# A batched matmul on one core: weights of four matrices in one load of 24 KB runs, their casts in quarter-lane pieces shared between VectorE and ScalarE

## Chip, cores, metric

One Trainium2 chip, one core, the other cores idle. The metric is the device time of one execution in microseconds (us), median of several. The kernel before takes 519.6 us, and its executions lie within 0.3 us.

## The reference

```python
b1, b2, m, k, n = 8, 16, 256, 512, 384
x:      (8, 16, 256, 512) float32
weight: (8, 16, 512, 384) float32
out = np.matmul(x, weight)            # 128 independent products, float32
```

The kernel reads 67.1 MB of x and 100.7 MB of weights and writes 50.3 MB. The products are made in bf16.

## The kernel before

Four matrices are a group, and there are 32 groups. SyncE issues all transfers, in program order: for group n + 4 the x and the two halves of the weights, then the store of group n. ScalarE casts x to bf16 and copies the products out of PSUM. TensorE transposes x and multiplies. VectorE casts the weights to bf16 and copies the transposed x.

```python
G = 4; C = P // G; R = G * M // P; T = R // 2      # P = 128, R = 8 rows a partition, T = 4
D = 2; S = 2; HP = P // D; NG = B // G             # half loads, half lanes, 32 groups
XS, WS, OS = 2, 2 * G // D, 4                      # buffers: x, half weights, out

def load(e, t, U, s):                              # SyncE
    n = t * U + s
    e.wait_ge(x_cast, n + (1 - XS))                # cut: only for n >= XS
    e.dma_start(x_sb[s % XS], ...)                 # 2 MB, 16 KB runs
    for d in range(G // D):
        e.wait_ge(w_cast, n * (G * S) + ((d + 1) * D * S - 2 * G * S))
        e.dma_start(w_sb[slot], ...)               # 1.5 MB, 12 KB runs, two matrices

def prepare(e, t, U, s):                           # VectorE
    for d in range(G // D):
        e.wait_ge(w_in[slot], ...)
        for a in range(D):
            for h in range(S):                     # 8 casts of 64 x 1536
                e.tensor_copy(out=w_bf[...][h * HP : (h + 1) * HP],
                              in_=w_sb[slot][a * HP : (a + 1) * HP, h * KO : (h + 1) * KO, :]
                              ).then_inc(w_cast, 1)
    for q in range(T):                             # 4 copies of the transposed x
        e.wait_ge(t_made, n * T + (q + 1 + BIAS))
        e.tensor_copy(out=x_t[...], in_=pt[...]).then_inc(t_copied, 1)

def step(t, U, s, more):                           # ScalarE
    for q in range(T):
        copy_out(e, t, U, s, q)                    # PSUM -> out_sb
        if q == 1 and more:
            cast_x(e, t, U, s + 1)                 # 2 casts of 128 x 2048
```

## Time and profile before

| | kernel before |
|---|---|
| time, us | 519.6 (519.5 to 519.8) |
| busy: VectorE, ScalarE, TensorE | 63%, 41%, 61% |
| packets' share of the DMA engines | 99.2% |
| issue to landing, us: x, half weights, store | 25.9, 27.6, 30.5 |

The prediction below shows the page's lines for this. Four groups of work are needed besides (columns: line, engine, operation, out<-in, shapes, count, busy us, mean ns, idle before and its releaser):

```profile
L148 DVE CAST w_bf<-w_sb 64x1536 bf16<-64x1536 f32 x256 | 244.4, 955 | 179.4 <-DMA w_sb<-in_weight_dram 172.3
...
L195 ACT COPY out_sb<-po 128x768 f32<-128x768 f32 x128 | 99.4, 803 | 291.0 <-PE po L181 291.0
...
L130 ACT CAST x_bf<-x_sb 128x2048 bf16<-128x2048 f32 x64 | 118.5, 1902 | 6.3 <-DMA x_sb<-in_x_dram 6.3
...
L154 DVE COPY x_t<-pt 128x1024 bf16<-128x1024 bf16 x128 | 79.5, 682 | 1.0
```

VectorE waits 172 us for weights and ScalarE 291 us for products: both have time to spare.

The **packet records** have size, start and duration of every DMA packet. The **landing records** have, for each transfer, one entry for each of the 16 DMA engines. From them I take when a transfer landed on the slowest engine (the last of 16, for which the program waits) and on the median engine (the eighth). The difference is called the **lag**. The records don't number the engines, so the last at one landing need not be the last at another; the table under e14 shows where that matters.

### The profile page before, as it was taken

The numbers are of one execution on the slowest core, as the hardware profiler recorded it, in microseconds if no ns is written. First come the engines' busy times: TensorE is split into PE (matmuls) and PEld (weight loads), VectorE is DVE, ScalarE is ACT, GpSimd is POOL, SyncE is SP. The second block draws the span as 40 slices with busy tenths as digits, with TensorE's granted clock in tenths as the row PEclk, the third lists the DMA queues.
The fourth block names the chain that finished last, engine by engine and source line by source line (L and its number), as shares of the span: only waits on it lengthen the run. The fifth ranks groups of instructions, "written<-read, shape, count | busy, mean of one in ns | idle before, by whom it ended". The sixth has DMA issues, their size and how long they took to land.

```text
span 518.0 us, 11228 instructions
## 1 busy us (share of the span) xinstructions
PE 315.0 (61%) x4608; PEld 198.0 (38%) x4608; DVE 323.9 (63%) x384; ACT 212.8 (41%) x193; POOL 0.7 (0%) x6
## 2 busy tenths in 40 slices
PE   0685775476655676555756557665566655675654
PEld 0453443343433443333434334343344333343432
DVE  0878867655577555775556765557755577555670
ACT  3073643455234552335542345423455234553242
POOL 0000000000000000000000000000000000000000
PEclk9798976888668776868786687768777787878687
DMA  8999999999999999999999999999999999999995
GB/s 337 430 424 428 426 429 427 430 428 427 430 429 426 431 425 430 428 430 432 426 427 429 430 433 425 427 430 428 432 429 427 427 430 430 430 429 424 432 428 229
DMA packets 18868, 218.16 MB, mean 421 GB/s; under 512 B 2096, under 2 KB 2096, under 8 KB 2608
## 3 DMA queue, kind: packets, MB, share of 16 engines
q1 hardware_dynamic: 18864, 218.11, 99.2%
q8 instruction: 2, 0.03, 0.0%
q14 instruction: 2, 0.02, 0.0%
HBM read 167.77 MB, written 50.33 MB: 421 GB/s over the span
## 4 chain that ended last, share of the span: by engine, by line
DMA 82%; DVE 13%; issue 2%; PE 2%; SPq 1%; ACT 0%; DVEq 0%
DMA w_sb<-in_weight_dram 82%; DVE w_bf L148 13%; PE po L181 2%; SPq L108 0%; SPq L100 0%; ACT out_sb L195 0%; DVE x_t L154 0%; DVEq L143 0%; DVEq L225 0%; SPq L287 0%; SPq L54 0%
## 5 line engine op out<-in xcount | busy, mean ns | idle before, releaser
L148 DVE CAST w_bf<-w_sb 64x1536 bf16<-64x1536 f32 x256 | 244.4, 955 | 179.4 <-DMA w_sb<-in_weight_dram 172.3
L181 PE MATMUL po<-w_bf,x_t 128*32 128x384 bf16 x4096 | 233.5, 402 | 122.2 <-DVE x_t L154 122.2
L195 ACT COPY out_sb<-po 128x768 f32<-128x768 f32 x128 | 99.4, 803 | 291.0 <-PE po L181 291.0
L181 PEld LDWEIGHTS po<-w_bf,x_t 128*32 128x32 bf16 x4096 | 125.8, 117 | 227.0 <-DVE x_t L154 131.7
L167 PE MATMUL pt<-identity,x_bf 128*128 128x128 f32 x512 | 81.5, 322 | 73.4 <-ACT x_bf L130 73.4
L130 ACT CAST x_bf<-x_sb 128x2048 bf16<-128x2048 f32 x64 | 118.5, 1902 | 6.3 <-DMA x_sb<-in_x_dram 6.3
L167 PEld LDWEIGHTS pt<-identity,x_bf 128*128 128x128 f32 x512 | 72.2, 212 | 85.2 <-issue 85.2
L154 DVE COPY x_t<-pt 128x1024 bf16<-128x1024 bf16 x128 | 79.5, 682 | 1.0
L130 ACT ACT_TABLE_LOAD x1 | 1.3, 1283 | 1.3 <-PEq L231 1.3
masks.py:199 POOL TENSOR_SCALAR_AFFINE_SELECT identity<-identity 128x128 f32<-128x128 f32 x1 | 0.3, 293 | 0.2 <-POOL identity L201 0.2
L201 POOL MEMSET identity<- 128x128 f32 x1 | 0.2, 205 | 0.5 <-SPq L54 0.5
L276 POOL MEMSET const-uint8-127<- 128x1 uint8 x1 | 0.1, 103 | 0.0
L276 POOL MEMSET const-bfloat16-1.0<- 128x1 bf16 x1 | 0.1, 102 | 0.0
L276 POOL MEMSET const-float32-0.0<- 128x1 f32 x1 | 0.1, 99 | 0.2 <-issue 0.2
L276 POOL MEMSET const-float32-1.0<- 128x1 f32 x1 | 0.1, 99 | 0.0
## 6 DMA issues: line engine op xcount, KB each, us to landing
w_sb<-in_weight_dram SPq DMA_DIRECT2D x64, 1536.0 KB, 27.6
x_sb<-in_x_dram SPq DMA_DIRECT2D x32, 2048.0 KB, 25.9
out_dram<-out_sb SPq DMA_DIRECT2D x31, 1536.0 KB, 30.5
out_dram<-out_sb SPq DMA_DIRECT2D x4, 384.0 KB, 4.1
```

Source lines behind the costliest of these rows:

```text
L130: ins = e.copy(out=x_bf[s % BS][:, :, h], in_=x_sb[s % XS][:].rearrange("p r (q s c) -> p r s q c", s=S, c=KO)[:, :, h],)
L148: e.tensor_copy(out=w_bf[(s * G + d * D + a) % WBS][h * HP : (h + 1) * HP], in_=w_sb[slot][a * HP : (a + 1) * HP, h * KO : (h + 1) * KO, : ...
L154: e.tensor_copy(out=x_t[s % TS][:, 2 * q : 2 * q + 2], in_=pt[(s * T + q) % PT][:].bitcast(bf16),).then_inc(t_copied, 1)
L167: ins = e.transpose(pt[(s * T + q) % PT][:, rr, h, :], words[:, 2 * q + rr, h :: KO // 2], identity[:],)
L181: ins = e.matmul(po[(s * T + q) % PO][mine, rr, :N], x_t[s % TS][:, 2 * q + rr, ko // 2, mine, ko % 2], w_bf[(s * G + i) % WBS][:, ko, :], ...
L195: e.copy(out=out_sb[s % OS][:, 2 * q : 2 * q + 2, :], in_=po[(s * T + q) % PO][:, :, :N],).then_inc(o_copied, 1)
L201: e.memset(identity[:], 0.0).then_inc(id_done, 1)
L276: nc = _bacc.Bacc("TRN2", target_bir_lowering=False, num_devices=1)
```

## The change

Intent: the DMA engines are the bound, so make their packets fewer and longer. With 16 rows of weights on each partition one load brings four matrices in runs of 24 KB. Each matrix then lies on 32 partitions, so it takes 16 casts of 32 lanes in place of 8 of 64. VectorE takes twelve. ScalarE takes four, of the next group, two before and two after its output copies, and casts x in four pieces between the copies. Weights are released for reload only when the whole group is cast. For the last group the weights are loaded before x.

```diff
-    XS, WS, OS = 2, 2 * G // D, 4
+    V = G - 1
+    XS, WS, OS = 2, 2, 4
-    w_sb = sbuf("w_sb", [P, S * KO, N], fp32, WS)
+    w_sb = sbuf("w_sb", [P, G * KO, N], fp32, WS)
+    def load_w(e, t, U, s):
+        n = t * U + s
+        if not isinstance(n, int) or n >= WS:
+            e.wait_ge(v_cast, (n - WS + 1) * (G * V))
+            e.wait_ge(a_cast, (n - WS + 1) * G)
+        e.dma_start(
+            w_sb[s % WS][:],
+            w_rows[bass.ds(n * (G * K), G * K)].rearrange("(p k) n -> p k n", k=G * KO),
+        ).then_inc(w_in[s % WS], 16)
+    def load(e, t, U, s):
+        order = (load_w, load_x) if isinstance(t, int) and s == NG - 1 else (load_x, load_w)
+        for part in order:
+            part(e, t, U, s)
+    def cast_w(e, cast, t, U, s, i, parts, done):
+        for h in parts:
+            cast(
+                out=w_bf[(s * G + i) % (2 * G)][h * C : (h + 1) * C],
+                in_=w_sb[s % WS][i * C : (i + 1) * C, h * KO : (h + 1) * KO, :],
+            ).then_inc(done, 1)
         # VectorE
+                for i in range(G):
+                    cast_w(e, e.tensor_copy, t, U, s, i, range(V), v_cast)
         # ScalarE
         def step(t, U, s, more):
+            if more:
+                casts(t, U, s + 1, (0, 1))
             for q in range(T):
                 copy_out(e, t, U, s, q)
-                if q == 1 and more:
-                    cast_x(e, t, U, s + 1)
+                if more:
+                    cast_x(e, t, U, s + 1, q)
+            if more:
+                casts(t, U, s + 1, (2, 3))
         # cut: on_sync leaves its loop a round earlier (groups 28 to 31 are
        # loaded by the unrolled end), cast_x by quarters, one x_bf and one x_t buffer for all groups,
         # waits on v_cast and a_cast in the matmuls
```

More of the change, by code (lines that the diff above doesn't have):

```diff
@@ L42 @@
     T = R // 2
-    D = 2
-    S = 2
-    HP = P // D
     NG = B // G
-    XS, WS, OS = 2, 2 * G // D, 4
-    BS, TS, WBS = 1, 2, 2 * G
+    V = G - 1
+    XS, WS, OS = 2, 2, 4
     PT, PO = 4, 2
@@ L71 @@
     x_sb = sbuf("x_sb", [P, R, K], fp32, XS)
-    x_bf = sbuf("x_bf", [P, R, S, HP, KO], bf16, BS)
-    x_t = sbuf("x_t", [P, R, KO // 2, P, 2], bf16, TS)
-    w_sb = sbuf("w_sb", [P, S * KO, N], fp32, WS)
-    w_bf = sbuf("w_bf", [P, KO, N], bf16, WBS)
+    x_bf = sbuf("x_bf", [P, R, G, C, KO], bf16, 1)[0]
+    x_t = sbuf("x_t", [P, R, KO // 2, P, 2], bf16, 1)[0]
+    w_sb = sbuf("w_sb", [P, G * KO, N], fp32, WS)
+    w_bf = sbuf("w_bf", [P, KO, N], bf16, 2 * G)
     out_sb = sbuf("out_sb", [P, R, N], fp32, OS)
@@ L79 @@
     po = psum("po", [P, 2, 512], fp32, PO)
-    id_done, x_cast, w_cast, t_made, t_copied, p_made, o_copied = (
+    id_done, x_cast, v_cast, a_cast, t_made, t_copied, p_made, o_copied = (
         sems(name, 1)[0]
         for name in (
-            "id_done", "x_cast", "w_cast", "t_made", "t_copied", "p_made", "o_copied"
+            "id_done", "x_cast", "v_cast", "a_cast",
+            "t_made", "t_copied", "p_made", "o_copied",
         )
@@ L93, with load_x @@
     BIAS = 8
-    def load(e, t, U, s):
+    def load_x(e, t, U, s):
         n = t * U + s
         if not isinstance(n, int) or n >= XS:
-            e.wait_ge(x_cast, n + (1 - XS))
+            e.wait_ge(x_cast, (n - XS + 1) * T)
         e.dma_start(
@@ L103, in load @@
         ).then_inc(x_in[s % XS], 16)
-        for d in range(G // D):
-            slot = (s * (G // D) + d) % WS
-            if not isinstance(n, int) or n >= 2:
-                e.wait_ge(w_cast, n * (G * S) + ((d + 1) * D * S - 2 * G * S))
-            e.dma_start(
-                w_sb[slot][:],
-                w_rows[bass.ds(n * (G * K) + d * (D * K), D * K)].rearrange(
-                    "(p k) n -> p k n", k=S * KO
-                ),
-            ).then_inc(w_in[slot], 16)
+    def load_w(e, t, U, s):
[11 more added lines that the diff above has]
+            part(e, t, U, s)
     def store(e, t, U, s, pieces=1):
@@ L123, in store, with cast_x, cast_w_start, evacuate @@
             )
-    def cast_x(e, t, U, s):
+    def cast_x(e, t, U, s, q):
         n = t * U + s
-        e.wait_ge(x_in[s % XS], (t * (U // XS) + s // XS) * 16 + 16)
-        e.wait_ge(t_made, n * T + ((1 - BS) * T + BIAS))
-        for h in range(S):
-            ins = e.copy(
-                out=x_bf[s % BS][:, :, h],
-                in_=x_sb[s % XS][:].rearrange("p r (q s c) -> p r s q c", s=S, c=KO)[
-                    :, :, h
-                ],
-            )
-        ins.then_inc(x_cast, 1)
-    def prepare(e, t, U, s):
+        if q == 0:
+            e.wait_ge(x_in[s % XS], (t * (U // XS) + s // XS) * 16 + 16)
+        e.wait_ge(t_made, n * T + (q + 1 - T + BIAS))
+        rows = slice(2 * q, 2 * q + 2)
+        e.copy(
+            out=x_bf[:, rows],
+            in_=x_sb[s % XS][:, rows].rearrange(
+                "p r (q s c) -> p r s q c", s=G, c=KO
+            ),
+        ).then_inc(x_cast, 1)
+    def cast_w(e, cast, t, U, s, i, parts, done):
[4 more added lines that the diff above has]
+            ).then_inc(done, 1)
+    def cast_w_start(e, t, U, s):
         n = t * U + s
         e.wait_ge(p_made, n * T + (BIAS - T))
-        for d in range(G // D):
-            slot = (s * (G // D) + d) % WS
-            e.wait_ge(
-                w_in[slot], (t * (U * G // D // WS) + s * G // D // WS) * 16 + 16
-            )
-            for a in range(D):
-                for h in range(S):
-                    e.tensor_copy(
-                        out=w_bf[(s * G + d * D + a) % WBS][h * HP : (h + 1) * HP],
-                        in_=w_sb[slot][a * HP : (a + 1) * HP, h * KO : (h + 1) * KO, :],
-                    ).then_inc(w_cast, 1)
+        e.wait_ge(w_in[s % WS], (t * (U // WS) + s // WS) * 16 + 16)
+    def evacuate(e, t, U, s):
+        n = t * U + s
         for q in range(T):
@@ L154, in prepare @@
             e.tensor_copy(
-                out=x_t[s % TS][:, 2 * q : 2 * q + 2],
+                out=x_t[:, 2 * q : 2 * q + 2],
                 in_=pt[(s * T + q) % PT][:].bitcast(bf16),
@@ L160, in multiply @@
         n = t * U + s
-        words = x_bf[s % BS][:].rearrange("p r s q c -> p r (s q c)").bitcast(fp32)
-        e.wait_ge(x_cast, n + 1)
+        words = x_bf[:].rearrange("p r s q c -> p r (s q c)").bitcast(fp32)
         for q in range(T):
+            e.wait_ge(x_cast, n * T + (q + 1))
             e.wait_ge(t_copied, n * T + (q + 1 - PT + BIAS))
@@ L172, in multiply @@
             ins.then_inc(t_made, 1)
-        e.wait_ge(w_cast, n * (G * S) + G * S)
+        e.wait_ge(v_cast, n * (G * V) + G * V)
+        e.wait_ge(a_cast, n * G + G)
         for q in range(T):
@@ L182, in multiply @@
                             po[(s * T + q) % PO][mine, rr, :N],
-                            x_t[s % TS][:, 2 * q + rr, ko // 2, mine, ko % 2],
-                            w_bf[(s * G + i) % WBS][:, ko, :],
+                            x_t[:, 2 * q + rr, ko // 2, mine, ko % 2],
+                            w_bf[(s * G + i) % (2 * G)][:, ko, :],
                             start=(ko == 0),
@@ L209, in on_sync @@
             load(e, 0, NG, n)
-        rounds = (NG - LAG) // U
+        rounds = (NG - LAG) // U - 1
         with e.Fori(0, rounds) as t:
@@ L226, in on_vector @@
             for s in range(U):
-                prepare(e, t, U, s)
+                cast_w_start(e, t, U, s)
+                for i in range(G):
+                    cast_w(e, e.tensor_copy, t, U, s, i, range(V), v_cast)
+                evacuate(e, t, U, s)
     def on_tensor(e):
@@ L242, in on_scalar, with casts @@
             e.sem_inc(o_out[s], 16)
+        def casts(t, U, s, group):
+            if group[0] == 0:
+                cast_w_start(e, t, U, s)
+            for i in group:
+                cast_w(e, e.copy, t, U, s, i, range(V, G), a_cast)
         def step(t, U, s, more):
+            if more:
+                casts(t, U, s + 1, (0, 1))
             for q in range(T):
                 copy_out(e, t, U, s, q)
-                if q == 1 and more:
-                    cast_x(e, t, U, s + 1)
-        cast_x(e, 0, NG, 0)
+                if more:
+                    cast_x(e, t, U, s + 1, q)
+            if more:
+                casts(t, U, s + 1, (2, 3))
+        for q in range(T):
+            cast_x(e, 0, NG, 0, q)
+        casts(0, NG, 0, (0, 1, 2, 3))
         with e.Fori(0, NG // U - 1) as t:
```

## The prediction

> **What bounds the kernel now.** I read the page first: busy shares, then the slices, then the chain of waits.
>
> ```profile
> span 518.0 us, 11228 instructions
> PE 315.0 (61%) x4608; PEld 198.0 (38%) x4608; DVE 323.9 (63%) x384; ACT 212.8 (41%) x193; POOL 0.7 (0%) x6
> DMA  8999999999999999999999999999999999999995
> GB/s 337 430 424 428 426 429 427 430 428 427 430 429 426 431 425 430 428 430 432 426 427 429 430 433 425 427 430 428 432 429 427 427 430 430 430 429 424 432 428 229
> q1 hardware_dynamic: 18864, 218.11, 99.2%
> DMA w_sb<-in_weight_dram 82%; DVE w_bf L148 13%; PE po L181 2%; SPq L108 0%; SPq L100 0%; ACT out_sb L195 0%; DVE x_t L154 0%; DVEq L143 0%; DVEq L225 0%; SPq L287 0%; SPq L54 0%
> ```
>
> No compute engine is above 63%. The 16 DMA engines are busy from the second slice to the second last, and packets fill 99.2% of their time. Only the two end slices are short: the first by (430-337)/430 of 12.95 us, 2.8 us, the last by 6.1 us. So there are three things to gain or lose: time per packet, gaps in the stream, and the two ends.
>
> Is the queue always full, or just full enough? The issues say:
>
> ```profile
> w_sb<-in_weight_dram SPq DMA_DIRECT2D x64, 1536.0 KB, 27.6
> x_sb<-in_x_dram SPq DMA_DIRECT2D x32, 2048.0 KB, 25.9
> out_dram<-out_sb SPq DMA_DIRECT2D x31, 1536.0 KB, 30.5
> ```
>
> A load lies 26 to 28 us behind others, more than the 16 us of a group (four matrices; 32 groups). The 82% of the chain on the weight loads is this queueing, not a slow load.
>
> In the packet records a 3,072 B packet takes 121 ns, 12,288 B 460, 16,384 B 611 (medians). The line through them is 7.2 ns + 0.03686 ns per byte. One group gives an engine 16 weight, 8 x and 8 store packets and four semaphore writes of 9 ns: 24 x 460 + 8 x 611 + 36 = 15,964 ns; the landings of x two groups apart differ by 31.98 us, 15.99 a group. The steady state is thus the sum of its packets.
>
> The engines are not equal. In the landing records one engine is 0.6 us behind the median engine at the first load, 1.5 at 34 us and 3.5 at 497 us. A load has landed when this engine is done. It decides the end too: the last load lands at 497.4; five stores of 3.69 us follow, 18.4 us, so 515.9 at the earliest; the last packet ends at 516.1, its landing is at 516.55, the span closes 1.45 us later. The compute chain after the last load was only just shorter:
>
> ```profile
> 493.85 7.86 DVE L148 CAST w_bf<-w_sb 64x1536 bf16<-64x1536 f32 x8 [5.64 <-DMA w_sb<-in_weight_dram]
> 501.74 2.48 DVE L154 COPY x_t<-pt 128x1024 bf16<-128x1024 bf16 x4
> 502.48 8.09 PE L181 MATMUL po<-w_bf,x_t 128*32 128x384 bf16 x128 [4.28 <-DVE x_t L154]
> 510.63 0.80 ACT L195 COPY out_sb<-po 128x768 f32<-128x768 f32 x1 [0.50 <-PE po L181]
> ```
>
> Casts, copies, matmuls and output copies follow each other; the last store is issued at 511.5 and lands on the median engine at 513.7. So before, this chain has some 3 us to spare behind the slow DMA engine.
>
> **What the Trainium skill says.** "DMA: Bandwidth & Descriptors", section "Why small descriptors are slow (HBM only)", puts a fixed cost of a few cycles on each packet. The trace agrees: 7.2 ns, 1.6% of a 12 KB packet, so little to win. "ScalarE: Activation LUTs", section "What ACT_TABLE_LOAD costs": 186 ns + 0.833 ns per element with immediate operands; for 2,048 elements 1,892, the trace has 1,902; pairs overlap by 52 ns here (3.70 us for two), where the page says about 93. "VectorE: DVE Perf Modes", section "Why `tensor_reduce` can't reduce along partition axis": each partition is an independent lane, so a cast on 32 lanes should cost what one on 64 costs. The trace of before has only 64-lane casts (955 ns, one each 983 ns), so this is a step on trust. Its section "Two Vector instructions with no wait between them" says that a changed start quadrant makes an instruction wait for all before it; all casts change it before and after, and the 28 ns gap is already in the 983.
>
> **The change, part by part.**
>
> (1) Packets. 8 packets of 24,576 B (7.2 + 906 = 913 ns, estimated on the line above) take the place of 16 of 460, and one semaphore write fewer: 7,360 + 9 - 7,304 = 65 ns a group, x 32 = -2.1 us. This is on the bound.
>
> (2) VectorE: 12 casts a group in place of 8, 12 x 0.983 = 11.8 us, and 2.5 for the four x_t copies: 14.3 of the 15.9 us of a group. Busy 384 x 0.955 + 79.5 = 446 us. Just under the bound.
>
> (3) ScalarE: four weight casts of 1,536 elements (186 + 1,280 = 1.47 us, 1.41 in a row), four x casts of 1,024 (1.04, 0.99 in a row) for two of 1.90, and four output copies (0.80, 0.75): 5.7 + 4.0 + 3.0 = 12.7 us of 15.9. Busy about 425 us for 212.8.
>
> (4) Does the stream stay full? Call L the landing of a group's weights. VectorE casts until L+11.9, ScalarE does two casts (L+2.9), four pairs of output copy and x cast (L+9.9), two casts (L+12.7). So x for two groups on is issued at about L+10, weights at L+12.8. What is queued by then, the next weights and a store, lasts until L+19.6, and the x after it until L+24.5. 9 to 11 us of slack: no gap in the steady state. Latency to landing falls to about 14 us for x and 19 for weights, and costs nothing.
>
> (5) Start. No stores are queued yet and the first groups run cast after cast: weights 0 land at 16.2, VectorE casts to 28, then 30.6 to 42.4 and 45 to 56.8. ScalarE finishes the x casts of group 2 at about 52; x 4 is issued then and its first packet comes about 1 us later, while weights 3 end at 52.5. Weights 4 wait for 56.8 and x 4 ends at about 58. I put the gaps at 0.8 us together, on the bound.
>
> (6) End. The last group's weights are now loaded before its x, but VectorE is still at the group before. From L of the second last weights: last weights land at 11.0, last x at 15.9. VectorE is free at 14.4, casts to 26.25, copies the first x_t by 27.0. ScalarE does two casts by 15.55, four output copies and x casts by 22.55, two casts by 25.4. Matmuls 27.05 to 35.15 (8.1 as before), copy to 35.95, store issued at 36.05, landed 2.1 later at 38.2. That is 22.3 us after the last load; before it was 516.55 - 497.41 = 19.1. The stores alone would still take 18.4 plus 0.7. So the end moves from the slow DMA engine to the compute chain and costs +3.1 us; faster matmuls, 7.6 as one group earlier, would make it 2.6. I take +2.9.
>
> Sum: -2.1 + 0.8 + 2.9 = +1.6 us. With 519.6 that is 521.2; the slow engine should drift less with half the weight packets, a few tenths, so 521.0.
>
> **Rivals.** (a) Long runs pay: a 24 KB packet costs less than the line says, or the end overlaps better. For: the edit is built around it. Against: three packet sizes lie on one line, and 430 GB/s is near the 435 which the skill's DMA page gives as the ceiling. Without part 6 the time would be 518.3. (b) 24 KB runs are split into two packets: part 1 vanishes, 523. (c) VectorE becomes the bound: its slack is 1.6 us a group, 10%. A 32-lane cast of 1.12 us instead of 0.98 would reach 16 us a group; each further 0.1 us costs 38 us in all. Nothing in the trace speaks for it (casts spread over 951 to 959 ns beside full DMA), but it has no 32-lane cast. (d) ScalarE's fixed order, which holds output copies behind a weight landing, starves PE and the queue: it has 3 us of slack a group and the queue 9 more, so only the start and end feel it; twice my start gap gives 522.
>
> **Range and chances.** The known terms are each 1 to 3 us and all mechanisms but (c) stay within 2% (10.4 us). The range is 518.2 to 524.5: low if the end costs nothing more, high if the packets win nothing and the start costs double. Faster by over 2%: 0.01; within: 0.96; slower: 0.03, all of it (c).
>
> **What would show it.** Packets fall from 18,868 to about 14,260 and the 24 KB ones take 913 ns (1). VectorE's casts stay at 955 ns, x384, ScalarE's weight casts 1.47 us, busy near 446 and 425 us (2, 3). Slices 3 to 38 stay at 428 to 432 GB/s (4), with a dip in slices 4 or 5 if (5) holds. The last slices fall more than before, and the time from the last x landing to the end grows from 20.6 to 23 or 24 us (6). I am wrong if VectorE is busy over 95%, if DMA dips in the middle, or if the end is no longer than before.

## The result, and the profile after

The changed kernel takes **526.4 us** (525.7 to 526.9, 4 runs) against 519.6. The ratio is 1.013, interval 1.011 to 1.015. Ratios are the mean time of one kernel's runs over that of the other's of the same rounds, so not quite the ratio of the medians. This lies above the range of the prediction, 518.2 to 524.5.

The page of the changed kernel:

```profile
span 524.7 us, 11696 instructions
...
PE 331.4 (63%) x4608; PEld 210.4 (40%) x4608; DVE 444.5 (85%) x512; ACT 409.2 (78%) x385; POOL 0.7 (0%) x6
...
DMA  8999899999999999999999999999999999999994
GB/s 342 432 425 397 348 409 412 432 423 433 435 427 429 428 431 438 430 429 426 431 430 437 428 429 431 427 431 438 431 428 428 435 431 437 428 428 395 375 415 190
DMA packets 14260, 218.16 MB, mean 416 GB/s; under 512 B 1584, under 2 KB 1584, under 8 KB 2096
...
q1 hardware_dynamic: 14256, 218.11, 98.1%
```

The rate has three holes: slices 4 to 7 (39 to 92 us, deepest in 4 and 5), slices 37 to 39 (472 to 511 us), and a last slice below the 229 of before. In between it is a little above that of before. The packets fell to the predicted 14,260. The groups answer to those above:

```profile
L144 DVE CAST w_bf<-w_sb 32x1536 bf16<-32x1536 f32 x384 | 365.0, 951 | 69.2 <-DMA w_sb<-in_weight_dram 56.5
...
L144 ACT CAST w_bf<-w_sb 32x1536 bf16<-32x1536 f32 x128 | 187.9, 1468 | 86.4 <-DMA w_sb<-in_weight_dram 80.8
...
L135 ACT CAST x_bf<-x_sb 128x1024 bf16<-128x1024 f32 x128 | 134.2, 1050 | 7.0 <-DMA x_sb<-in_x_dram 6.3
L200 ACT COPY out_sb<-po 128x768 f32<-128x768 f32 x128 | 102.4, 800 | 16.9 <-PE po L186 16.1
```

A 32-lane cast takes what a 64-lane cast took (951 and 955 ns), and every duration is as predicted. VectorE and ScalarE still wait for the loads, so neither has become the bound. The issues show what got smaller, the time that a load lies in the queue:

```profile
w_sb<-in_weight_dram SPq DMA_DIRECT2D x32, 3072.0 KB, 18.6
x_sb<-in_x_dram SPq DMA_DIRECT2D x32, 2048.0 KB, 14.4
out_dram<-out_sb SPq DMA_DIRECT2D x31, 1536.0 KB, 21.8
```

The 24,576 B packets take 912 ns (median), as worked out. So where do 6.7 us of the span come from? The landing records answer, in us, slowest engine / median engine:

| landed | before | after | later by |
|---|---|---|---|
| weights 3 | 53.97 / 52.41 | 54.48 / 52.92 | 0.5 / 0.5 |
| weights 4 | 66.22 / 64.69 | 69.39 / 68.70 | 3.2 / 4.0 |
| x 8 | 123.06 / 120.93 | 127.01 / 125.21 | 4.0 / 4.3 |
| store 26 | 485.18 / 481.66 | 489.94 / 484.13 | 4.8 / 2.5 |
| both last loads | 497.41 / 493.88 | 503.63 / 498.93 | 6.2 / 5.1 |
| last store | 516.55 / 513.68 | 523.27 / 523.18 | 6.7 / 9.5 |

Read the slowest engine, for which the program waits. It loses 3.2 us by 69 us, 1.6 between weights 4 and store 26, 1.5 at the last loads and 0.5 at the end. The median engine wins 1.8 us back between x 8 and store 26, which fits the packet saving. The slowest engine wins nothing there: its lag grows from 1.8 to 5.8 us.

The first hole, by stretches of the two traces (columns: stretch, length, busy us and count of PE, PEld, DVE, ACT, POOL, granted clock, DMA share, GB/s). Before:

```profile
38.00:51.00 13.00, 7.47 (x108) 4.76 (x104) 10.74 (x13) 4.99 (x5) 0.00 (x0) 0.87 1.00 425
51.00:57.00 6.00, 4.02 (x79) 2.88 (x72) 5.81 (x7) 5.80 (x5) 0.00 (x0) 1.00 1.01 429
57.00:75.00 18.00, 12.78 (x208) 8.35 (x210) 13.82 (x18) 7.40 (x7) 0.00 (x0) 0.81 1.01 428
```

After:

```profile
38.00:51.00 13.00, 8.74 (x133) 4.72 (x133) 12.63 (x16) 10.67 (x11) 0.00 (x0) 0.74 0.99 399
51.00:57.00 6.00, 2.43 (x20) 2.05 (x16) 5.82 (x7) 5.93 (x6) 0.00 (x0) 0.86 0.59 205
57.00:75.00 18.00, 13.61 (x196) 8.14 (x200) 17.54 (x22) 16.40 (x16) 0.00 (x0) 0.78 1.01 411
```

From 51 to 57 us the DMA engines are idle for 2.2 us (the share of 0.59 counts a packet where it starts; this figure is from the packets cut at the ends of the stretch), because x 4 is issued only at 53.59 us, behind ScalarE's casts. But the stretches beside it show full shares at 399 and 411 GB/s. There the packets themselves are longer: near 39 us, after x 3 was issued at 38.34 us; when the engines start again near 54 us, up to 1,764 ns for 16 KB (611 in the steady state); and once more near 66 us, up to 1,655 ns for 24 KB. Together that is 2.1 us an engine between 30 and 70 us, against 0.3 before. A share of 1.0 is thus no proof of a full rate: look at GB/s beside it.

The end (start, duration, what, idle before it):

```profile
500.49 11.74 DVE L144 CAST w_bf<-w_sb 32x1536 bf16<-32x1536 f32 x12
...
510.11 2.96 ACT L144 CAST w_bf<-w_sb 32x1536 bf16<-32x1536 f32 x2
...
512.27 2.48 DVE L158 COPY x_t<-pt 128x1024 bf16<-128x1024 bf16 x4
...
513.41 6.68 PE L186 MATMUL po<-w_bf,x_t 128*32 128x384 bf16 x128 [2.46 <-ACT w_bf L144]
...
520.14 0.80 ACT L200 COPY out_sb<-po 128x768 f32<-128x768 f32 x1 [0.50 <-PE po L186]
```

VectorE and ScalarE finish the last casts almost together. Most DMA engines have nothing to do meanwhile (17% share from 513 to 518 us), while the slowest still works on store 30 until 519.3 and then lands the four pieces of the last store 0.97 us apart without a pause. The compute chain and the slowest engine reach the end together.

### The profile page after: what moved, and what is told of

Same layout as the page of the kernel before. It is cut to its first block, busy times and chain, and to the rows that moved or that the text cites. A ratio compares the mean times of both kernels' runs of the same rounds, so it can differ in the third digit from the quotient of the medians. Undisturbed runs are those within 1.5% of the kernel's fastest.

```text
span 524.7 us, 11696 instructions
## 1 busy us (share of the span) xinstructions
PE 331.4 (63%) x4608; PEld 210.4 (40%) x4608; DVE 444.5 (85%) x512; ACT 409.2 (78%) x385; POOL 0.7 (0%) x6
## 4 chain that ended last, share of the span: by engine, by line
DMA 49%; ACT 19%; issue 13%; PE 9%; DVE 9%; ACTq 0%; SPq 0%; DVEq 0%
DMA w_sb<-in_weight_dram 49%; ACT w_bf L144 10%; PE po L186 8%; DVE w_bf L144 7%; ACT out_sb L200 5%; ACT x_bf L135 4%; DVE x_t L158 2%; PE pt L171 1%; ACTq L199 0%; SPq L108 0%; ACTq L133 0%; ACTq L271 0%; SPq L98 0%; DVEq L230 0%; SPq L107 0%
## 5 line engine op out<-in xcount | busy, mean ns | idle before, releaser
L144 DVE CAST w_bf<-w_sb 32x1536 bf16<-32x1536 f32 x384 | 365.0, 951 | 69.2 <-DMA w_sb<-in_weight_dram 56.5
L186 PE MATMUL po<-w_bf,x_t 128*32 128x384 bf16 x4096 | 251.3, 415 | 161.0 <-ACT out_sb L200 64.3
L144 ACT CAST w_bf<-w_sb 32x1536 bf16<-32x1536 f32 x128 | 187.9, 1468 | 86.4 <-DMA w_sb<-in_weight_dram 80.8
L186 PEld LDWEIGHTS po<-w_bf,x_t 128*32 128x32 bf16 x4096 | 142.1, 118 | 261.6 <-DVE x_t L158 102.0
L135 ACT CAST x_bf<-x_sb 128x1024 bf16<-128x1024 f32 x128 | 134.2, 1050 | 7.0 <-DMA x_sb<-in_x_dram 6.3
L200 ACT COPY out_sb<-po 128x768 f32<-128x768 f32 x128 | 102.4, 800 | 16.9 <-PE po L186 16.1
L171 PEld LDWEIGHTS pt<-identity,x_bf 128*128 128x128 f32 x512 | 68.3, 208 | 47.7 <-issue 46.3
```

What stands on the lines that cost most here:

```text
L135: e.copy(out=x_bf[:, rows], in_=x_sb[s % XS][:, rows].rearrange("p r (q s c) -> p r s q c", s=G, c=KO),).then_inc(x_cast, 1)
L144: cast(out=w_bf[(s * G + i) % (2 * G)][h * C : (h + 1) * C], in_=w_sb[s % WS][i * C : (i + 1) * C, h * KO : (h + 1) * KO, :],).then_inc(do ...
L171: ins = e.transpose(pt[(s * T + q) % PT][:, rr, h, :], words[:, 2 * q + rr, h :: KO // 2], identity[:],)
L186: ins = e.matmul(po[(s * T + q) % PO][mine, rr, :N], x_t[:, 2 * q + rr, ko // 2, mine, ko % 2], w_bf[(s * G + i) % (2 * G)][:, ko, :], sta ...
L200: e.copy(out=out_sb[s % OS][:, 2 * q : 2 * q + 2, :], in_=po[(s * T + q) % PO][:, :, :N],).then_inc(o_copied, 1)
```

## The experiments

Fourteen kernels in all, every one correct. Before each, what was expected of it.

### First theory: three holes, each with its own cause

**e1: x before weights in the last group too.**

```diff
-        order = (load_w, load_x) if isinstance(t, int) and s == NG - 1 else (load_x, load_w)
+        order = (load_x, load_w)
```

> Undo one part: the last group loads x before its weights, like all others. Main theory (the 6.8 us are a gap of 3 to 4 us near 53 us, a gap with slow packets of 1.5 to 2.6 us near 483 us, and a slowest DMA engine that gains nothing from the longer packets): the last x is asked for some 3 us earlier, so the dip near 483 us goes and both last loads are in about 1.5 us earlier; but the weights now come last and VectorE needs 11.75 us for them, so the time from the last load to the end grows from 19.6 to 21 or 23 us. Together 525.5 to 528. Rival (the order of the last two loads has nothing to do with that dip; the casts are late anyway): the dip stays, and the time grows by 2 us or more, over 528.5.

Measured 528.3 us. The dip near 483 us is gone; the changed kernel first, then e1:

```profile
482.00:487.00 5.00, 2.79 (x64) 1.84 (x64) 3.33 (x6) 2.21 (x2) 0.00 (x0) 1.00 0.85 315
...
482.00:487.00 5.00, 4.11 (x60) 2.67 (x64) 3.30 (x5) 2.07 (x3) 0.00 (x0) 0.66 1.03 442
```

Both last loads are in at 501.37 on the slowest engine, 2.3 us earlier. Of this 0.8 us was there at weights 30 already, before the edit could act. From the last load to the last landing it takes 23.1 us in place of 19.6, as VectorE now starts the last casts late. So the dip does come from the order: the weights of group 31 wait for the casts of group 29, and x 31 stands behind them. The order of the changed kernel costs about 1.4 us there, wins 3.5 at the end, and is right.

**e2: the store ahead of the loads.**

```diff
-                load(e, t, U, LAG + s)
-                store(e, t, U, s)
+                store(e, t, U, s)
+                load(e, t, U, LAG + s)
```

(and the same in the unrolled end)

> Store of a group is issued ahead of the loads that wait for casts, not behind them. Main theory: store 0 was ready at about 37.5 us and fills the gap at 52 to 55 us, so the landing of store 0 and of the weights of group 4 both lie at 69 to 70 us, as in the kernel before, and the time falls by about 3 us to 522.5 to 524.5. Rival (the first groups' casts set the pace, the gap is only moved to the next load): the time stays within 0.7 us of 526.4.

Measured 528.0 us, a miss. The hole at 51 to 57 us is filled (share 0.96). Up to weights 30 with the stores before it the slowest engine was 2.2 us better off than in the changed kernel, and then the last x had a store in front of it and the end took it back.

**e3: the same kernel with 12 KB runs.**

```diff
-        e.dma_start(w_sb[s % WS][:], ...).then_inc(w_in[s % WS], 16)
+        for half in (slice(0, G * KO // 2), slice(G * KO // 2, G * KO)):
+            e.dma_start(w_sb[s % WS][:, half, :], rows[:, half, :]).then_inc(w_in[s % WS], 16)
```

(w_in is waited for at twice the count)

> The changed kernel, but the weights of a group in two transfers of 12 KB runs into the same buffer; all else as changed. If the packet saving lies on the bound, as predicted: +2.1 us, about 528.5. If the slowest DMA engine sets the pace and gains nothing from long packets, as its landings suggest: within 0.7 us of 526.4, with the median engine some 2 us later in the middle of the run than with 24 KB.

Measured 527.5 us, +1.0, between the two; the runs of the two kernels overlap (527.2 to 529.6, and 525.7 to 527.9 with e8), so the time alone proves little. The landings are cleaner. From x 8 to x 30, 22 groups, a group takes:

| us a group, x 8 to x 30 | median engine | slowest engine | growth of the lag, us |
|---|---|---|---|
| before (12 KB) | 15.895 | 15.957 | 1.36 |
| changed (24 KB) | 15.815 | 15.994 | 3.94 |
| e3, changed with 12 KB | 15.885 | 16.055 | 3.74 |

Long runs are worth 0.061 us a group on the slowest engine (0.052 from x 16 to x 28) and 0.070 on the median; 0.065 had been worked out. So my reading of the result, "the slowest engine wins nothing", was wrong in its cause: it wins its 2 us or a little less in 32 groups, and something else in the change takes them and more.

**e4: all four weight casts of ScalarE behind the output copies.**

```diff
-            if more:
-                casts(t, U, s + 1, (0, 1))
             for q in range(T):
                 copy_out(e, t, U, s, q)
                 ...
-                casts(t, U, s + 1, (2, 3))
+                casts(t, U, s + 1, (0, 1, 2, 3))
```

> ScalarE does the four output copies and x casts first and then all four weight casts, in place of two weight casts, copies and x casts, two weight casts. Main theory (x of group 4 comes late because its buffer is freed by x casts that stand behind two weight casts of 2.96 us): x 4 is issued near 50.6 in place of 53.6 us, the gap at 52 to 55 us shrinks to under 0.5 us, and the time falls to 523 to 524. Rival (VectorE's casts, done at 56.7 us, hold the next weights, and the gap moves there): the time falls by under 1 us.

Measured 550.8 us, a miss on both theories: the edit made a new bound. ScalarE in the middle of that run:

```profile
300.70 5.95 ACT L144 CAST w_bf<-w_sb 32x1536 bf16<-32x1536 f32 x4
309.79 0.80 ACT L200 COPY out_sb<-po 128x768 f32<-128x768 f32 x1 [3.14 <-PE po L186]
...
316.72 5.94 ACT L144 CAST w_bf<-w_sb 32x1536 bf16<-32x1536 f32 x4
325.81 0.80 ACT L200 COPY out_sb<-po 128x768 f32<-128x768 f32 x1 [3.14 <-PE po L186]
```

Casts to 306.65, matmuls that needed them, 3.14 us of waiting, copies, casts again: a ring through ScalarE and TensorE of 16.0 us a lap, 16.4 on average, over the 15.9 of DMA. With two casts ahead of the copies, as in the change, the ring is cut. ScalarE's busy time is 75% here and says nothing of this.

### Second theory: the start costs 3 us and can be had back

**e5: weights first in group 0 as well.** The order test becomes `s in (0, NG - 1)`.

> The changed kernel, with weights ahead of x in the load of the first group as well. Theory after the first four runs (the start gap comes because VectorE's casts, 11.75 us a group, can begin only when the whole 24 KB runs of group 0 have landed at 16.1 us, and everything of groups 0 to 3 follows from that): weights 0 land at 11.3 us, x of group 4 is issued near 51.5 in place of 53.6 us, the gap at 52 to 55 us shrinks from 2.2 us to under 0.5 us, and the time falls to 523.5 to 525. Rival (VectorE has to wait for weights 1 anyway, and the end swallows what the start wins, as with the store ahead): within 0.7 us of 526.4.

Measured 526.0 us, the rival's case. x 4 was issued at 51.2 us as expected, but the stretch from 51 to 57 us still reads 294 GB/s:

```profile
51.00:57.00 6.00, 2.77 (x32) 1.65 (x36) 5.84 (x9) 5.80 (x5) 0.00 (x0) 0.62 0.84 294
...
482.00:487.00 5.00, 4.47 (x64) 2.63 (x64) 3.28 (x5) 2.11 (x2) 0.00 (x0) 0.66 0.88 327
487.00:500.00 13.00, 8.46 (x116) 5.84 (x120) 12.65 (x15) 12.55 (x13) 0.00 (x0) 0.85 0.99 382
```

The median engine won 2 us at the start. It then ran dry a little longer near 482 us, because buffers come free only when the slowest engine, 6.5 us behind, has landed.

**e6: weights first in all groups.** The order is always `(load_w, load_x)`.

> Weights ahead of x in every group. If the losses are where I put them, the start gap falls to about 1 us (weights of group 4 are issued near 52.4 us), the dip near 483 us goes because weights have some 3 us more slack, and the second last weights land 20.8 in place of 15.9 us before the last x, so the chain of casts at the end starts earlier: 521 to 523.5. If the structure itself (casts on two engines, slower release of buffers) costs the time: over 525.5.

Measured 528.1 us, a miss. The lag of the slowest engine grew to 8.8 us at x 30, the most of all runs. Holes at the start remained (slices 3 to 5 at 407, 394 and 374 GB/s).

**e7: store first in the loop, loads first in the last part.** The first hunk of e2 alone.

> Store ahead of the loads in the loop, loads ahead of the stores in the last part as changed. In the run with the store ahead everywhere, the stream was 2.0 us less behind up to group 30 and lost it at the end, where the last x had a store in front of it. Theory: here the 2 us stay, 524 to 525. Rival (the chain at the end has a fixed distance from the start, not from the DMA stream, so nothing can be kept): 526 to 527.

Measured 526.4 us, a miss. The hole moved to where the order changes back:

```profile
430.00:436.00 6.00, 2.81 (x24) 2.14 (x16) 5.84 (x7) 5.78 (x6) 0.00 (x0) 1.00 0.88 335
436.00:482.00 46.00, 32.17 (x432) 20.30 (x432) 40.89 (x48) 37.23 (x36) 0.00 (x0) 0.81 1.00 406
```

So the second theory falls: e2, e5 and e7 each made the start better and none the time by more than 0.5 us. With this little slack in the queue a hole that is filled opens again at the next place where the order asks for a load early.

**e8: the changed kernel unaltered.**

> The changed kernel unaltered, for the spread: 525.7 to 527. If the drift of the slowest DMA engine is a trait of this kernel, it is again some 2 us behind the median engine at 200 us and over 5 us at 480 us; if it was chance of that run, it is elsewhere between 3.5 and 6.

Measured 526.5 us (526.3 to 527.9). The lag was 2.0 us at 198 us and 5.9 at 486. The drift is a trait of the kernel.

**e9: all casts on VectorE.** V = G, and no weight casts on ScalarE.

> The changed kernel with all 16 quarter-lane casts of a group on VectorE and none on ScalarE: the long runs without the sharing. 16 x 0.98 + 2.5 = 18.2 us of VectorE a group, over the 15.9 us of DMA, so VectorE becomes the bound: about 16 + 32 x 18.2 + 9 = 607 us, VectorE over 95% busy. If the queue or the DMA engines set the pace whatever the casts cost: under 540.

Measured 611.9 us; VectorE is a little less busy than expected:

```profile
PE 319.1 (52%) x4608; PEld 195.7 (32%) x4608; DVE 566.7 (93%) x640; ACT 217.8 (36%) x257; POOL 0.7 (0%) x6
```

A group takes 18.24 us. VectorE is the bound at 93% busy; of the rest 15.9 us are the waits for weights, nearly all at the start, and some 18 us the 28 ns gaps between its 640 instructions. The long runs need the sharing.

### Third theory: what makes one DMA engine fall back

Two suspects are left: the shallower queue and VectorE's work. Both can be put into the kernel before, alone.

**e10: the kernel before with later loads.**

```diff
+        if not isinstance(n, int):
+            e.wait_ge(p_made, n * T + (BIAS - T))     # ahead of the loads of group n
```

> The kernel before, but the loads of a group are issued only when the matmuls of the group two before are done. Nothing else changes; the queue is as shallow as in the changed kernel (x 13 to 16 us from issue to landing in place of 25.9) and still never empty in the steady state. If a shallow queue is what makes the slowest DMA engine fall back (from 2.0 us behind the median at 200 us to 5.7 at 480 in the changed kernel, from 2.1 to 3.5 before): lag over 5 us at 480 us and the time up by 1.5 to 3 us. If the drift comes from something else in the changed kernel: lag near 3.5 us, time within 0.7 us of 519.7.

Measured 523.7 us (521.9 to 525.3, the widest of all). The queue is shallower than in the changed kernel:

```profile
w_sb<-in_weight_dram SPq DMA_DIRECT2D x64, 1536.0 KB, 17.1
x_sb<-in_x_dram SPq DMA_DIRECT2D x32, 2048.0 KB, 11.8
```

Yet the lag grew by 1.37 us from x 8 to x 30, as before the change (1.36). The shallow queue does not make the drift. The time comes from elsewhere, and this I had not expected: the late loads open a hole at the start here too.

```profile
51.00:57.00 6.00, 3.34 (x48) 2.52 (x36) 5.81 (x7) 4.41 (x4) 0.00 (x0) 1.00 0.79 281
57.00:75.00 18.00, 10.89 (x160) 6.83 (x164) 13.36 (x18) 6.60 (x6) 0.00 (x0) 0.76 1.00 403
```

1.3 us idle, 1.9 us of longer packets from 45 to 70 us. The median engine was 3.1 us late at weights 4 and at weights 30; the slowest was 2.9 and 2.5 us late, and 2.5 at its last landing. A start hole of this kind does cost about 2.5 us of the profiled run's time, in a kernel that has nothing else of the change. The profiled run, 522.2 us, is one of the two fastest of six; why others lose up to 3 us more is not shown.

**e11: the kernel before with 12 casts on VectorE**, every second cast cut into two of 32 lanes.

```diff
                 for h in range(S):
-                    e.tensor_copy(...).then_inc(w_cast, 1)
+                    step = HP // 2 if h else HP
+                    for c in range(0, HP, step):
+                        ins = e.tensor_copy(...)      # lanes c to c + step
+                    ins.then_inc(w_cast, 1)
```

> The kernel before, with every second weight cast cut into two of 32 lanes: 12 casts a group on VectorE as in the changed kernel, 12 KB runs, 64-lane halves otherwise, ScalarE unaltered. If more casts and quarter lanes disturb the slowest DMA engine, or the longer chain of casts at the end costs: lag over 5 us at 480 us, time up by 2 us or more. If VectorE's share has nothing to do with the drift: lag near 3.5 us; the chain at the end is 3.9 us longer against 2.9 us of slack, so +0.5 to +1.5 us.

Measured 523.0 us. The lag grew by 4.33 us (6.0 at x 30), the slowest engine's group took 16.079 us in place of 15.957, the median's 15.882. No hole anywhere, and 3.3 us lost. The slowest engine was 2.5 us late at the landing of the last weights and 2.8 at its last landing. (The casts at the end take 3.9 us longer here as well, which uses up their slack of some 3 us: 2.5 of the 2.8 us go with the drift, the rest is theirs.)

**e12 and e13: the other way, two and four of the eight casts on ScalarE.**

```diff
+                if d * D + a < G - NA:              # NA = 1 (e12) or 2 (e13); VectorE
+                    cast_w(e.tensor_copy, s, slot, d, a, w_cast)
 ...
             for q in range(T):
                 copy_out(e, t, U, s, q)
                 ...
+            if more:
+                scalar_casts(e, t, U, s + 1)        # ScalarE, after its last copy
```

> The kernel before, with two of a group's eight 64-lane weight casts on ScalarE (after its last output copy of the group before) and six on VectorE. Theory (the more VectorE casts, the further one DMA engine falls back: 8 casts 3.45 us at 480 us, 12 casts 6.0): lag 2.5 to 3.2 us at 480 us, and the chain of casts at the end 1.4 us shorter, 518.3 to 519.3, a little faster than the kernel before. Rival (the drift has to do with the 32-lane form or with the time of the stores, not with VectorE's share): lag 3.3 to 3.6 us, time within 0.3 us of 519.7.

Measured 519.3 us against 519.7, ratio 0.9992, interval 0.9977 to 1.0006: the same. The lag was 3.1 us at x 30, but it grew by 1.44 us from x 8, no less than with eight casts. The theory of a drift in step with the number of casts is not borne out below eight.

> As the last, with four of the eight casts on ScalarE and four on VectorE. Theory: lag 1.5 to 2.7 us at 480 us; the casts at the end are done at 503.1 in place of 501.7 us, which is inside the slack of 2.9 us, so 517.8 to 519.2. Rival: lag 3.3 to 3.6 us and time 519.5 or more; if ScalarE's casts slow the DMA engine just as VectorE's do, the same.

Measured 566.2 us, inconclusive for the drift: four casts behind ScalarE's copies closed the ring of e4 (17.1 us a group), and with the DMA engines no longer the bound the lag stays at 1.8 us.

**e14: the kernel before with four spare 64-lane casts**, into a buffer that nobody reads.

```diff
+                e.tensor_copy(
+                    out=spare[d * D + a][HP:P],
+                    in_=w_sb[slot][a * HP : (a + 1) * HP, KO : 2 * KO, :],
+                ).then_inc(spared, 1)
                 for h in range(S):
```

> The kernel before with four more 64-lane casts a group on VectorE, into a spare buffer that nobody reads: 12 casts a group as in the changed kernel, but none of 32 lanes. If the number (or time) of VectorE's casts makes the slowest DMA engine fall back: the lag grows by about 4 us between the landings of x 8 and x 30, as with 12 casts of which 8 are of 32 lanes (4.33), and the time is near 523. If it is the 32-lane form: the lag grows by 1.2 to 1.6 us, as with 8 or 6 casts of 64 lanes (1.36, 1.44), and the time is 519.5 to 521.5 (the chain of casts at the end is longer).

Measured 522.8 us, and the lag grew by 3.34 us: nearer to 4 than to 1.4. So the growth goes with the four more casts and not with the 32-lane form. The casts, from this run's trace:

```profile
L155 DVE CAST w_bf<-w_sb 64x1536 bf16<-64x1536 f32 x256 | 244.4, 955 | 8.0
...
L150 DVE CAST spare<-w_sb 64x1536 bf16<-64x1536 f32 x128 | 122.3, 956 | 55.5 <-DMA w_sb<-in_weight_dram 52.2
```

The growth from x 8 to x 30 mixes two engines. Lags at x 8, 12, 16, 20, 24 and 28 are 2.13, 2.09, 2.29, 2.62, 2.96, 3.32 us before and 1.80, 2.03, 2.43, 3.29, 4.00, 4.83 after. In these two runs, up to about x 14, the last engine is one that stays a fixed time behind; it then shows as the second slowest, still near 2 us (1.92 before and 2.06 after at x 28). Another engine, which falls back by the same amount every group, has overtaken it. Its rate is read from x 16 to x 28, with no hole between:

| | VectorE casts a group | slowest engine, us a group, x 8 to x 30 | growth of the lag, x 8 to x 30, us | growth a group, x 16 to x 28, us | time, us |
|---|---|---|---|---|---|
| e12 | 6 of 64 lanes | 15.954 | 1.44 | 0.076 | 519.3 |
| before | 8 of 64 | 15.957 | 1.36 | 0.085 | 519.7 |
| e10, late loads | 8 of 64 | 15.958 | 1.37 | 0.081 | 523.7 |
| e14 | 12 of 64 | 16.038 | 3.34 | 0.195 | 522.8 |
| e11 | 4 of 64, 8 of 32 | 16.079 | 4.33 | 0.191 | 523.0 |
| changed, 24 KB | 12 of 32 | 15.994 | 3.94 | 0.200 | 526.4 |
| e3, changed with 12 KB | 12 of 32 | 16.055 | 3.74 | 0.181 | 527.5 |
| e6, weights first | 12 of 32 | 16.135 | 7.10 | 0.331 | 528.1 |

The rates fall into two groups, about 0.08 us with six or eight casts and 0.18 to 0.20 with twelve, whatever their form and the packets' length. At the landing of the last weights the slowest engine is 2.5 us (e11) and 2.6 us (e14) late. But e6 has the same casts as the changed kernel and only another order of loads, and drifts by 0.331. So the number of casts is not all: more casts, like another order, also move the times at which transfers and casts meet, and no run separates the two.

The packet records go with it in part. In the kernel before, between 100 and 440 us, of the 12 KB packets that lie wholly within a run of VectorE's casts 31 of 3,315 take over 480 ns, of those with no cast beside them 0 of 4,473. In e11 it is 82 of 4,734 and 0 of 2,736. But in e12, with nearly the drift of before, it is only 6 of 3,384, and in the changed kernel, where 12 KB packets are stores, 59 of 698 and 21 of 1,796. So long packets beside casts are not the whole of the drift.

No version here beats the kernel before by more than the spread; e12 equals it.

## Why the prediction was wrong, point by point

The sign was right and the packet term was right. The sum, +1.6 us, was wrong in four terms (points 3 to 6); on the slowest engine +6.7 us were measured. The end, taken 2.4 us too long, hides part of what the other three lack; that was luck.

1. **Packets, -2.1 us: right.** 912 ns a packet; e3 gives 0.052 to 0.061 us a group on the slowest engine, 1.7 to 2.0 in 32 groups. But the 15.99 us a group that I took as proof that the steady state is the sum of its packets was the slowest engine's; the median engine takes 15.895.
2. **VectorE and ScalarE below the bound: right.** Busy 444.5 and 409.2 us (446 and 425 predicted). A pair of ScalarE's weight casts takes 2.96 us; I had let them overlap, 2.82. And a pair of x casts, 1,902 ns each and 3.70 us together, overlaps by 102 ns, not by the 52 that I read. The two errors nearly cancel.
3. **"The slow engine should drift less with half the weight packets": wrong, the largest error in kind.** Its lag grew by 3.94 us in place of 1.36. I had treated VectorE's extra casts as work beside the DMA. e11 and e14, with no edit but to VectorE's casts, raise the drift from 0.085 to 0.19 us a group, and their slowest engine is 2.5 and 2.6 us late at the last weights. That uses up the packet term: between weights 4 and store 26 the slowest engine lost 1.6 us, where -1.4 were expected (22 groups at 0.065). I had also taken the lagging engine for one and the same; it is one at a fixed distance first and a drifting one later.
4. **Start, +0.8 us: too small; 3.2 on the slowest engine, 4.0 on the median.** The cause was the predicted one. x 4 was issued at 53.6 us, not 52, as output copies waited for matmuls (1.1 and 0.7 us). And I counted only idle time, which was 2.2 us. The long packets around the hole, 1.8 us more than before, were not in the sum at all; e10 shows the same pair, 1.3 idle and 1.9 long packets, in another kernel.
5. **"9 to 11 us of slack: no gap in the steady state": right there, wrong for the last group.** I reckoned the slack from the slowest engine's landings, but the median engine is 5.7 us ahead of it. Weights 31 were issued 13.4 us after weights 29 had landed; the median engine had work for about 19.6 - 5.7 = 13.9 us less the time to the first packet. The swapped order put x 31, ready 3 us earlier, behind that wait. The hole near 483 us and its long packets cost 1.5 us; e1 removes the hole.
6. **End, +2.9 us: too large; 0.5.** The matmuls began 9.8 us after the last x in place of 11.15 and took 6.7 in place of 8.1 us. The last copy ended at 520.9 us, 17.3 after the last x, where 20.05 were expected. The late loads had given VectorE and ScalarE more of a lead: VectorE began its last casts 3.1 us before the last x landed, where 1.5 had been reckoned.

Shown by edits: 1, 2 (e9), in 3 that four more casts more than double the drift, the order's part in 5. For 4, e10 shows what such a hole costs, and e2, e5 and e7 that filling it moves it. What the changed kernel lacks beside that is the 26 us of queue of the kernel before: a load waits for a whole group's casts, 13 us after landing. No version undoes the drift or the start within the changed kernel and gets the time back, so how the 6.7 us divide is read from landings and not from a repair.

**Left open.** By what path VectorE's casts slow one DMA engine, or whether it is the times of the transfers that they shift; which engine it is; and why six casts do hardly better than eight. Why packets are long a second time some 12 us after a restart (near 54 and 66 us, 484 and 496, in e7 433 and 445). And why weights first everywhere (e6), with the same casts, made the drift worst.

## What to carry to other kernels

When 16 DMA engines are the bound, look at the slowest of them: the program waits for its landings, and its lag eats the slack that the queue seems to have. A longer run saves only the fixed cost of a packet, here 7 ns in 460, and it is easily outweighed if the layout it needs holds buffers longer or puts more casts on VectorE. Reckon a hole in a full stream at more than its idle time (1.3 us idle cost 2.5 to 3.1 in e10), and draw the ring of waits before moving work within an engine's order: in e4 and e13 no compute engine was over 82% and 71% busy, and they lost 24 and 47 us.

## What the Trainium skill lacked or had wrong

- "SBUF — State Buffer", section "SBUF: two separate sides", says that a DMA cannot be slowed by a compute operation. Here four more VectorE casts a group raised the time a group takes on the slowest of the 16 DMA engines from 15.957 to 16.038 us (e14) and 16.079 (e11), with all transfers issued from SyncE. That the casts act on the transfers themselves, and not by shifting their times, is not shown.
- "DMA: Bandwidth & Descriptors" puts two usually slower engines down, as a best guess, to descriptor rings of transfers issued from GpSimd (section "Latency and other measured facts"). No transfer here is issued from there, and in the runs that the DMA engines bound to the end one engine is still 2.9 (e10) to 8.8 us (e6) behind the median at x 30, while the second and third slowest stay at 1.9 and 1.7 us (before, x 28). Our records do not number them.
- No page looked at tells the cost of a queue that runs dry: after 1.3 us of idle time packets took 1.9 us longer in sum on each engine, part of it some 12 us later (e10).
- "ScalarE: Activation LUTs", section "What ACT_TABLE_LOAD costs", gives an overlap of about 93 ns for consecutive instructions. A pair of x casts agrees (102 ns: 1,902 each, 3.70 us for two), but ScalarE's weight casts overlap with nothing: on 32 lanes 24 ns lie between two of them (1,468 ns each, 2.96 us for two). Why is not shown.
